# Decoder layer on one core: the relu of the index scores stays in its PSUM bank, and the weighted sum reads it from there

## The chip, the cores and the metric

One core of one Trainium2 chip runs the whole program. The metric is the device time of one launch in microseconds (us). The kernel before took 1060.78 us, the median of three runs (1059.88 to 1061.40). The profile comes from one further execution, of 1061.52 us.

## What is computed

One layer in float32: 512 tokens of width 1024 go through a SwiGLU feed-forward block, a token mixer of two head groups, and a second SwiGLU block. The change lies in the mixer's first group, where a small indexer scores every earlier key for every query and each query keeps its best 128 keys:

```python
idx_logits = jnp.einsum('bqhd,bsd->bqhs', qib, k_idx)       # 16 index heads of width 64
score = jnp.einsum('bqh,bqhs->bqs', wb, jax.nn.relu(idx_logits))
score = jnp.where(causal[None], score, -jnp.inf)
_, sel = lax.top_k(score, top_k)                            # top_k = 128
```

The first block of 128 queries sees no more than 128 keys, so it needs no scores. The blocks 1, 2 and 3 score 256, 384 and 512 keys.

## The kernel before

The program is written with pools of named tiles, and a scheduler puts the instructions of each engine into an order and adds the waits. Engines run their own queues in that order: TensorE (PE) the matmuls, ScalarE (ACT) activations, VectorE (DVE) elementwise work, GpSimd (POOL) part of the elementwise work, SyncE (SP) the issue of transfers. PSUM has eight banks of 128x512 float32, all handed out by one helper (`acc`, which is also `sc` and `tr`; line 77); a matmul group takes a free bank and must wait where none is free.

A float32 matrix product is made of three matmuls on operands split into a high and a low part (`mm3`, line 135). The weights are split by `split` (line 93): an ACT copy writes the high part (line 94), DVE or POOL subtracts it from the raw weights to get the low part (line 95). The set ON_VECTOR says which of these subtractions, and which additions of the rotary embedding, are DVE's; the others are POOL's.

The mixer's first part is written out by hand in the string ORDER: `q0` to `q7` project index queries for two heads each (`index_queries`), `s0` to `s7` rotate them and split them into stacked tiles (`rope`, lines 622 to 636, and `stack`, lines 644 to 654; four transfers on SP move quarters of the low part, line 639), `i0` to `i7` make the scores of two heads each (`index_heads`), `l0` to `l4` project the latents of the second head group (`latent`, lines 736 to 746), and `b` stands for rounds of the selection (`topk`).

For each of 16 heads and 3 blocks, so 48 times, `index_heads` does this:

- two matmuls put the scores of 128 queries against 256, 384 or 512 keys into a bank `p` (lines 707 and 708),
- ACT writes the relu of the bank into an SBUF tile `r`, one of four (line 710),
- DVE multiplies `r` by the head's weight per query and adds the sum so far, `score[i]`, which the trace calls idx (line 711). For the first head it adds the mask cmask instead.

The bank is free again when the relu is done. The tile `r` is free when the sum is done.

`topk` then takes the eight largest scores of each row (line 719) and replaces them (line 720), 16 rounds for the three blocks, all on DVE, and line 723 turns the result into a mask for the attention. `latent` reads its product three times: ACT writes the scaled high part (line 741), DVE the low part (line 742), ACT the squares for the norm (line 154). Line 872 is the first step of the attention's softmax.

Of the kernel before, what the change touches and what calls it, by code (L numbers as in the profile page):

```python
# [11 lines left out]
AF = mybir.ActivationFunctionType  # L12
# [561 lines left out]
def mixer(k, mp, mix, ids, xs, turn_rest, norm, tabs, g_q, g_kv, row_tile, out_done, on_token):  # L574
    nc = k.nc
# [3 lines left out]
    fr = lambda: pp.tile([P, T], F32, tag="r", name=k.name("r"), bufs=BUFS["pr"])  # L579
# [85 lines left out]
    wt = mp.tile([P, NT, 16], F32, tag="wt", name="wt", bufs=1)  # L665
    qst = lambda: mp.tile([P, T], F32R, tag="kf", name=k.name("qst"), bufs=8)
    score = {i: mp.tile([P, T], F32, tag="idx", name=f"idx_{i}", bufs=3)[:, :(i + 1) * P] for i in range(1, NT)}
# [32 lines left out]
    def index_heads(c, stacks):  # L700
        for j, s in enumerate(stacks):
            h = 2 * c + j
            for i in range(1, NT):
                n = (i + 1) * P
                p = k.sc()[:, :n]
                q = s[:, (i - 1) * P:i * P]
                nc.tensor.matmul(p, q, kih[:, :n], start=True, stop=False)
                nc.tensor.matmul(p, q, kil[:, :n], start=False, stop=True)
                r = fr()[:, :n]
                nc.scalar.activation(r, p, AF.Relu)  # L710
                nc.vector.scalar_tensor_tensor(out=score[i], in0=r, scalar=wt[:, i, h:h + 1],  # L711
                                               in1=cm(i) if h == 0 else score[i], op0=ALU.mult, op1=ALU.add)


# [124 lines left out]
    def values_b(j):  # L839
        wv = k.weights(ids["V"])  # L840
        for j in range(NT):
            p = k.acc()
            for a in range(2):
# [5 lines left out]

    do = dict(T=keys, c=norm_column, t=rest, r=norm_rows, k=index_keys, a=attention_keys, v=rest_out, w=lambda j: values(v.x2),  # L850
              e=lambda j: rotary_key(v.x2), q=index_queries, s=index_stack, i=lambda j: index_heads(j, stacks.pop(j)), l=latent,
              K=keys_b, R=keys_b_out, p=rotary_b, u=rotary_b_out, n=nope, A=queries_a, S=stack_a, V=values_b, b=background)
    for w in steps[:steps.index("|")]:
# [379 lines left out]
```

## Time and profile before

| | |
|---|---|
| median of three runs | 1060.78 us |
| profiled execution, whole | 1061.52 us |
| its span, first to last instruction | 1059.7 us |
| mean granted TensorE clock | 0.987 |
| PE busy, share of the span | 1016.4 us, 96% |
| DVE busy | 513.2 us, 48% |
| ACT busy | 384.3 us, 36% |
| POOL busy | 147.5 us, 14% |
| index scores, first matmul to last sum | 416.2 to 478.0 us |
| selection, line 719 to line 723 | 478.6 to 549.8 us |

The shares are means over stages that differ. Before 380 us and after 660 us the feed-forward blocks keep PE busy in nearly every slice; in between, the mixer loads DVE and POOL far more, and what bounds it has to be read from that stretch alone. A busy PE is no proof of a bound: an instruction's time there is modelled and overlaps the next one's. Rows in order of time merge neighbours of one group (a last field "x3" says three instructions) and give start, duration and, in brackets, the idle time just before and who ended it.

### The profile page before, as it was taken

The numbers are of one execution on the slowest core, as the hardware profiler recorded it, in microseconds if no ns is written. First come the engines' busy times: TensorE is split into PE (matmuls) and PEld (weight loads), VectorE is DVE, ScalarE is ACT, GpSimd is POOL, SyncE is SP. The second block draws the span as 40 slices with busy tenths as digits, with TensorE's granted clock in tenths as the row PEclk, the third lists the DMA queues.
The fourth block names the chain that finished last, engine by engine and source line by source line (L and its number), as shares of the span: only waits on it lengthen the run. The fifth ranks groups of instructions, "written<-read, shape, count | busy, mean of one in ns | idle before, by whom it ended". The sixth has DMA issues, their size and how long they took to land.

```text
span 1059.7 us, 12214 instructions
## 1 busy us (share of the span) xinstructions
PE 1016.4 (96%) x4726; PEld 829.8 (78%) x4726; DVE 513.2 (48%) x897; ACT 384.3 (36%) x689; POOL 147.5 (14%) x142
## 2 busy tenths in 40 slices
PE   6999999999999999889879999999999999999997
PEld 4888888888888888768755567888888888888886
DVE  6433333233332346989996767553333233333343
ACT  5422222122222335563466556442222211222232
POOL 1000000000000026625975122000000000000000
PEclk9999999999999999989988999999999999999999
DMA  8322332233313123333350001344323232222302
GB/s 278 120 80 81 118 119 80 80 99 109 111 60 97 40 80 109 114 92 98 98 174 15 2 19 43 102 138 124 113 80 119 80 113 86 80 83 98 119 0 80
DMA packets 83390, 98.84 MB, mean 93 GB/s; under 512 B 9026, under 2 KB 65474, under 8 KB 83332
## 3 DMA queue, kind: packets, MB, share of 16 engines
q1 hardware_dynamic: 83328, 98.06, 29.4%
q8 instruction: 37, 0.61, 0.2%
q14 instruction: 21, 0.17, 0.1%
q10 hardware_dynamic: 4, 0.00, 0.0%
HBM read 91.89 MB, written 2.10 MB: 89 GB/s over the span
## 4 chain that ended last, share of the span: by engine, by line
PE 80%; DVE 12%; issue 3%; ACT 3%; POOL 1%; DMA 1%; SPq 0%; POOLq 0%; ACTq 0%; DVEq 0%
PE ps L137 24%; PE ps L140 24%; PE ps L141 24%; DVE idx L720 2%; DVE s L719 2%; DVE idx L711 1%; PE ps L960 1%; DVE wl L95 1%; PE ps L998 1%; DVE p L892 1%; PE ps L993 1%; PE ps L957 1%; DVE p L872 1%; PE ps L982 1%; DVE f L626 0%
## 5 line engine op out<-in xcount | busy, mean ns | idle before, releaser
L94 ACT ACTIVATE wh<-raw 128x1024 fp32r<-128x1024 f32 (+4 forms) x154 | 140.1, 925 | 381.1 <-PE ps L140 298.9
L95 DVE TENSOR_TENSOR wl<-raw,wh 128x1024 fp32r<-128x1024 f32 (+1 forms) x122 | 145.5, 1196 | 266.2 <-ACT wh L94 265.9
L137 PE MATMUL ps<-xh,wh 128*128 128x512 f32 (+2 forms) x712 | 265.9, 378 | 5.1 <-DVE res L1137 1.7
L141 PE MATMUL ps<-xh,wl 128*128 128x512 f32 (+2 forms) x712 | 267.3, 377 | 1.2 <-POOL wl L95 0.9
L140 PE MATMUL ps<-xh,wh 128*128 128x512 f32 (+2 forms) x712 | 267.2, 377 | 0.5 <-DVE xh L95 0.5
L137 PEld LDWEIGHTS ps<-xh,wh 128*128 128x128 f32 x712 | 133.7, 189 | 29.6 <-DVE f L629 2.1
L141 PEld LDWEIGHTS ps<-xh,wl 128*128 128x128 f32 x712 | 134.6, 189 | 24.9 <-POOL wl L95 1.3
L140 PEld LDWEIGHTS ps<-xh,wh 128*128 128x128 f32 x712 | 134.5, 189 | 23.6 <-DVE xh L95 0.7
L137 PE MATMUL ps<-wh,h 128*128 128x512 f32 x272 | 105.9, 389 | 0.0
L140 PE MATMUL ps<-wl,h 128*128 128x512 f32 x272 | 105.8, 389 | 0.0
L141 PE MATMUL ps<-wh,h 128*128 128x512 f32 x272 | 105.8, 389 | 0.0
L95 POOL TENSOR_TENSOR wl<-raw,wh 128x512 fp32r<-128x512 f32 (+5 forms) x32 | 43.3, 1374 | 394.4 <-ACT wh L94 389.8
L334 DVE TENSOR_TENSOR t<-ps,t 128x512 f32<-128x512 f32 x44 | 30.4, 691 | 138.5 <-PE ps L141 138.5
L94 ACT ACTIVATE w<-raw 128x1024 fp32r<-128x1024 f32 x32 | 33.9, 1061 | 117.5 <-PE ps L140 117.5
L137 PE MATMUL ps<-xh,w 128*128 128x512 f32 x176 | 68.5, 389 | 0.0
L141 PE MATMUL ps<-xh,w 128*128 128x512 f32 x176 | 68.5, 389 | 0.0
L140 PE MATMUL ps<-xh,w 128*128 128x512 f32 x176 | 68.5, 389 | 0.0
L289 POOL TENSOR_TENSOR fr<-tot,mhalf 128x1 f32<-128x1 f32 x12 | 7.0, 582 | 417.9 <-DVE tot L1180 360.1
L140 PEld LDWEIGHTS ps<-wl,h 128*128 128x128 f32 x272 | 51.1, 188 | 10.6
L141 PEld LDWEIGHTS ps<-wh,h 128*128 128x128 f32 x272 | 51.1, 188 | 10.6
L137 PEld LDWEIGHTS ps<-wh,h 128*128 128x128 f32 x272 | 51.0, 188 | 10.6
L95 DVE TENSOR_TENSOR w<-raw,w 128x1024 fp32r<-128x1024 f32 x32 | 39.2, 1225 | 29.8 <-ACT w L94 29.8
(214 smaller groups left out, 1346.2 us busy)
## 6 DMA issues: line engine op xcount, KB each, us to landing
raw<-in_w_up_dram SPq DMA_DIRECT2D x22, 1024.0 KB, 5.3
raw<-in_w_gate_dram SPq DMA_DIRECT2D x21, 1024.0 KB, 5.3
raw<-in_w_down_dram SPq DMA_DIRECT2D x20, 1024.0 KB, 5.0
raw<-in_w_in_dram SPq DMA_DIRECT2D x8, 1024.0 KB, 5.2
raw<-in_w_out_dram SPq DMA_DIRECT2D x4, 1024.0 KB, 5.8
res<-in_x_dram SPq DMA_DIRECT2D x4, 512.0 KB, 6.0
raw<-in_w_down_dram SPq DMA_DIRECT2D x4, 512.0 KB, 3.8
raw<-in_w_ukv_dram SPq DMA_DIRECT2D x2, 1024.0 KB, 4.9
```

Source lines behind the costliest of these rows:

```text
L94: i = self.nc.scalar.activation(hi, src, AF.Copy)
L95: (lo_engine or self.nc.vector).tensor_tensor(out=lo, in0=src, in1=hi.bitcast(F32), op=ALU.subtract)
L137: i = mm(out, wh, xh, start=first, stop=False)
L140: mm(out, wh, xl, start=False, stop=False)
L141: return i, mm(out, wl, xh, start=False, stop=last)
L334: nc.vector.tensor_tensor(out=u, in0=pu, in1=g, op=ALU.mult)
L711: nc.vector.scalar_tensor_tensor(out=score[i], in0=r, scalar=wt[:, i, h:h + 1], in1=cm(i) if h == 0 else score[i], op0=ALU.mult, op1=ALU.add)
L719: nc.vector.max(out=m8, in_=score[i])
L720: nc.vector.match_replace(out=score[i], in_to_replace=m8, in_values=score[i], imm_value=TAKEN)
L872: nc.vector.tensor_tensor_reduce(out=e, in0=p[:, :n], in1=bias, scale=1.0, scalar=-3.0e38, op0=ALU.add, op1=ALU.max, accum_out=mx[:, c:c + 1])
L892: nc.vector.tensor_scalar(out=e, in0=e, scalar1=rc[:, c:c + 1], scalar2=None, op0=ALU.mult)
L957: nc.tensor.transpose(p[:, i * P:(i + 1) * P], probs[i][:, j * P:(j + 1) * P], k.ident)
```

## The change

The tile `r` is gone. The relu writes back into the bank that it reads, and the weighted sum takes its first operand from that bank. The bank is therefore free only when the sum is done. The same 48 relus and 48 sums run. The pool's four `r` buffers remain allocated (one call, line 657, stays).

```diff
--- before.py
+++ after.py
@@ -706,9 +706,8 @@
                 q = s[:, (i - 1) * P:i * P]
                 nc.tensor.matmul(p, q, kih[:, :n], start=True, stop=False)
                 nc.tensor.matmul(p, q, kil[:, :n], start=False, stop=True)
-                r = fr()[:, :n]
-                nc.scalar.activation(r, p, AF.Relu)
-                nc.vector.scalar_tensor_tensor(out=score[i], in0=r, scalar=wt[:, i, h:h + 1],
+                nc.scalar.activation(p, p, AF.Relu)
+                nc.vector.scalar_tensor_tensor(out=score[i], in0=p, scalar=wt[:, i, h:h + 1],
                                                in1=cm(i) if h == 0 else score[i], op0=ALU.mult, op1=ALU.add)
```

Line numbers behind line 709 are smaller by one after the change. The scheduler orders the queues anew. On TensorE the order of the index part is the same, but the matmuls that open a bank wait for another engine. Below are the widest score of one index head and all three of the next, at the end of a run of 12 scores that closes with a latent projection; ps is a bank, kih and kil the split index keys, qst a stacked query tile, and the brackets name the queues whose semaphore is waited for (Activation is ACT). Before:

```order
L707 MATMUL ps_3361<-kih,qst_3198 128x512 [waits Activation_49]
L708 MATMUL ps_3361<-kil,qst_3198 128x512
L707 MATMUL ps_3367<-kih,qst_3199 128x256 [waits DMAHW1_49,DMAHW0_49,Activation_49]
L708 MATMUL ps_3367<-kil,qst_3199 128x256
L707 MATMUL ps_3373<-kih,qst_3199 128x384 [waits Activation_49]
L708 MATMUL ps_3373<-kil,qst_3199 128x384
L707 MATMUL ps_3379<-kih,qst_3199 128x512 [waits Activation_49]
L708 MATMUL ps_3379<-kil,qst_3199 128x512
L137 MATMUL ps_3389<-xh_2392,wh_3145 128x512 [waits Activation_49]
```

After:

```order
L707 MATMUL ps_3329<-kih,qst_3180 128x512 [waits DVE_49]
L708 MATMUL ps_3329<-kil,qst_3180 128x512
L707 MATMUL ps_3334<-kih,qst_3181 128x256 [waits DMAHW7_49,DMAHW0_49,DVE_49]
L708 MATMUL ps_3334<-kil,qst_3181 128x256
L707 MATMUL ps_3339<-kih,qst_3181 128x384 [waits Activation_49]
L708 MATMUL ps_3339<-kil,qst_3181 128x384
L707 MATMUL ps_3344<-kih,qst_3181 128x512 [waits DVE_49]
L708 MATMUL ps_3344<-kil,qst_3181 128x512
L137 MATMUL ps_3353<-xh_2392,wh_3127 128x512 [waits DVE_49]
```

The rows are the same matmuls in the same places. Before, a bank is handed on when ACT is done with it, after the change in most places when DVE is.

On ScalarE, from the last scores of the third pair of heads to the first of the fourth (f and qst are the rotated queries and their stack, wh the high part of weights). Before:

```order
L94 ACTIVATE wh_3100<-raw_3098 128x1024
L710 ACTIVATE r_3089<-ps_3086 128x384
L648 ACTIVATE qst_3135<-f_3129 128x384
L650 ACTIVATE qst_3136<-f_3129 128x384
L710 ACTIVATE r_3095<-ps_3092 128x512
L94 ACTIVATE wh_3145<-raw_3098 128x1024
L648 ACTIVATE qst_3182<-f_3174 128x384
L650 ACTIVATE qst_3183<-f_3174 128x384
L94 ACTIVATE wh_3278<-raw_3276 128x1024
L710 ACTIVATE r_3243<-ps_3240 128x256
```

After:

```order
L709 ACTIVATE ps_3075<-ps_3075 128x512
L648 ACTIVATE qst_3117<-f_3111 128x384
L650 ACTIVATE qst_3118<-f_3111 128x384
L94 ACTIVATE wh_3082<-raw_3080 128x1024
L94 ACTIVATE wh_3127<-raw_3080 128x1024
L648 ACTIVATE qst_3164<-f_3156 128x384
L650 ACTIVATE qst_3165<-f_3156 128x384
L94 ACTIVATE wh_3254<-raw_3252 128x1024
L709 ACTIVATE ps_3222<-ps_3222 128x256
```

Before, the last relu of the third pair stands behind a weight split and behind the copies of queries; after, it stands ahead of both, as no buffer `r` has to come free.

On VectorE at the same place (idx_2657 to idx_2659 are the three blocks' sums, wl the low part of weights, h the low part of queries). Before:

```order
L711 SCALAR_TENSOR_TENSOR idx_2657<-r_3083,wt,idx_2657 128x256
L95 TENSOR_TENSOR wl_3101<-raw_3098,wh_3100 128x1024
L711 SCALAR_TENSOR_TENSOR idx_2658<-r_3089,wt,idx_2658 128x384
L711 SCALAR_TENSOR_TENSOR idx_2659<-r_3095,wt,idx_2659 128x512
L626 TENSOR_TENSOR f_3192<-ps_3104,tab_2644 128x384
L628 TENSOR_TENSOR f_3193<-ps_3104,tab_2645 64x384
L629 TENSOR_TENSOR f_3193<-ps_3104,tab_2645 64x384
L626 TENSOR_TENSOR f_3210<-f_2842,tab_2648 128x512
L649 TENSOR_TENSOR h_3184<-f_3174,qst_3182 128x384
```

After:

```order
L710 SCALAR_TENSOR_TENSOR idx_2659<-ps_3060,wt,idx_2659 128x512
L710 SCALAR_TENSOR_TENSOR idx_2657<-ps_3065,wt,idx_2657 128x256
L710 SCALAR_TENSOR_TENSOR idx_2658<-ps_3070,wt,idx_2658 128x384
L710 SCALAR_TENSOR_TENSOR idx_2659<-ps_3075,wt,idx_2659 128x512
L95 TENSOR_TENSOR wl_3083<-raw_3080,wh_3082 128x1024
L626 TENSOR_TENSOR f_3174<-ps_3086,tab_2644 128x384
L628 TENSOR_TENSOR f_3175<-ps_3086,tab_2645 64x384
L629 TENSOR_TENSOR f_3175<-ps_3086,tab_2645 64x384
L626 TENSOR_TENSOR f_3192<-f_2842,tab_2648 128x512
L649 TENSOR_TENSOR h_3166<-f_3156,qst_3164 128x384
```

The weight split (line 95) stood ahead of the last two sums of that pair and now stands behind them; the rotary steps (lines 626 to 629) follow in the same order. On SyncE, two loads of weights (the last latent's, and the query weights of the second group) now stand behind two and four more of the copies of line 639. All other queues keep their order but for swaps of neighbours.

## Rows read from the trace of the kernel before

**Rows 1.** chain of work that ended last, whole span, shares by engine.

```profile
PE 80%; DVE 12%; issue 3%; ACT 3%; POOL 1%; DMA 1%; SPq 0%; POOLq 0%; ACTq 0%; DVEq 0%
```

**Rows 2.** busy us per engine in stretches; PEclk, DMA share, GB/s close each row.

```profile
472.00:500.00 28.00, 27.95 (x136) 23.29 (x134) 28.00 (x72) 12.97 (x26) 11.01 (x11) 1.00 0.30 97
...
500.00:520.00 20.00, 17.58 (x85) 14.24 (x86) 20.00 (x55) 7.23 (x13) 19.36 (x15) 1.00 0.37 113
...
520.00:550.00 30.00, 24.85 (x110) 18.88 (x108) 29.94 (x63) 17.34 (x26) 27.17 (x23) 0.96 0.48 140
```

**Rows 3.** VectorE groups by form, 420 to 480 us: busy us, mean ns of one, idle.

```profile
L711 DVE SCALAR_TENSOR_TENSOR idx<-r,wt,idx 128x512 f32<-128x512 f32 x15 | 14.8, 985 | 0.0
...
L711 DVE SCALAR_TENSOR_TENSOR idx<-r,wt,idx 128x384 f32<-128x384 f32 x15 | 11.9, 796 | 0.1
...
L711 DVE SCALAR_TENSOR_TENSOR idx<-r,wt,idx 128x256 f32<-128x256 f32 x15 | 10.0, 667 | 0.0
...
L742 DVE SCALAR_TENSOR_TENSOR lat<-ps,g_q_lat,lat 128x512 fp32r<-128x512 f32 x2 | 1.5, 747 | 2.0 <-ACT lat L741 2.0
...
L711 DVE SCALAR_TENSOR_TENSOR idx<-r,wt,cmask 128x512 f32<-128x512 f32 x1 | 0.7, 744 | 0.0
...
L711 DVE SCALAR_TENSOR_TENSOR idx<-r,wt,cmask 128x384 f32<-128x384 f32 x1 | 0.6, 611 | 0.0
...
L711 DVE SCALAR_TENSOR_TENSOR idx<-r,wt,cmask 128x256 f32<-128x256 f32 x1 | 0.5, 485 | 1.4 <-ACT r L710 1.4
```

**Rows 4.** VectorE in order of time, 425 to 444 us: start, duration, what.

```profile
425.79 2.65 DVE L711 SCALAR_TENSOR_TENSOR idx<-r,wt,idx 128x512 f32<-128x512 f32 x2
...
428.83 1.96 DVE L711 SCALAR_TENSOR_TENSOR idx<-r,wt,idx 128x384 f32<-128x384 f32 x3
...
434.50 3.20 DVE L711 SCALAR_TENSOR_TENSOR idx<-r,wt,idx 128x384 f32<-128x384 f32 x3
...
439.58 4.16 DVE L711 SCALAR_TENSOR_TENSOR idx<-r,wt,idx 128x384 f32<-128x384 f32 x2
```

**Rows 5.** GpSimd in order of time, two weight splits.

```profile
440.48 2.71 POOL L95 TENSOR_TENSOR wl<-raw,wh 128x1024 fp32r<-128x1024 f32 x1
...
469.04 2.40 POOL L95 TENSOR_TENSOR wl<-raw,wh 128x1024 fp32r<-128x1024 f32 x1 [7.34 <-ACT wh L94]
```

**Rows 6.** VectorE in order of time, 459 to 473 us.

```profile
459.99 7.55 DVE L711 SCALAR_TENSOR_TENSOR idx<-r,wt,idx 128x256 f32<-128x256 f32 x12
...
469.57 0.75 DVE L742 SCALAR_TENSOR_TENSOR lat<-ps,g_q_lat,lat 128x512 fp32r<-128x512 f32 x1 [2.03 <-ACT lat L741]
...
470.24 3.05 DVE L711 SCALAR_TENSOR_TENSOR idx<-r,wt,idx 128x256 f32<-128x256 f32 x2
```

**Rows 7.** who waited for whom, 415 to 480 us: total us, times, longest.

```profile
ACT r L710 <- DVE idx L711: 9.5, 8, 3.3
...
PE ps L707 <- DMA qst<-h: 4.0, 2, 3.0
...
PEld ps L707 <- ACT r L710: 2.2, 3, 1.2
```

**Rows 8.** TensorE matmuls in order of time, four rows of 457 to 513 us.

```profile
457.38 0.55 PE L707 MATMUL ps<-kih,qst 128*128 128x256 f32 x1 [2.99 <-DMA qst<-h]
...
459.05 0.69 PE L707 MATMUL ps<-kih,qst 128*128 128x384 f32 x1 [0.90 <-ACT r L710]
...
472.37 0.50 PE L137 MATMUL ps<-xh,wh 128*128 128x512 f32 x1
...
512.97 0.50 PE L137 MATMUL ps<-xh,wh 128*128 128x512 f32 x1 [1.54 <-ACT wh L94]
```

**Rows 9.** who waited for whom, 480 to 500 us.

```profile
ACT f L154 <- DVE lat L742: 9.6, 3, 3.4
```

**Rows 10.** ScalarE group by form, 420 to 480 us, the widest relu.

```profile
L710 ACT ACTIVATE r<-ps 128x512 f32<-128x512 f32 x16 | 9.7, 605 | 4.8 <-DVE idx L711 3.9 <-PE ps L708 0.8
```

**Rows 11.** SyncE queue in order of time, one row.

```profile
447.41 2.41 SPq L639 DMA_DIRECT2D qst<-h  x4
```

## The prediction

> **What bounds the kernel now.** I started from the chain of waits that ended last: PE carries 80% of it and DVE 12% [rows 1]. The reader is to see that a DVE change can only pay where DVE stands in that chain, so next I looked at busy time by stretch [rows 2]. From 472 to 500 us DVE is busy 28.00 of 28.00 us, to 520 us 20.00 of 20.00, to 550 us 29.94 of 30.00. PE is just as full until 500 us (27.95), then has gaps; POOL is nearly full from 500 us on (19.36 of 20, 27.17 of 30). So DVE bounds the selection, with PE and POOL close behind, and time saved on DVE ahead of 478 us can move the whole rest of the program, as far as those two follow.
>
> Then I asked what DVE's weighted sums cost, by form [rows 3]. The sums of the first head take 744, 611 and 485 ns for 512, 384 and 256 columns. The other 45, with the same work, average 985, 796 and 667 ns. In order of time the long ones stand together [rows 4]: two sums from 439.58 us take 4.16 us, and the POOL split that runs from 440.48 us takes 2.71 us of it [rows 5]. DVE and POOL evidently hold each other up when both read two operands from SBUF. The low part of a latent is the same DVE operation, with its first operand in PSUM: its row at 469.57 us takes 0.75 us although a POOL split runs from 469.04 us for 2.40 us; the two sums right behind it, with both operands in SBUF, take 3.05 us [rows 5, 6].
>
> **The change, part by part.** *The sums.* With `p` in place of `r` a sum has one operand in SBUF and one in PSUM, like that latent row, and I take it that POOL no longer holds it up. Saved on DVE: 15 x (985 - 744) + 15 x (796 - 611) + 15 x (667 - 485) ns = 3.6 + 2.8 + 2.7 = 9.1 us [rows 3]. Reading PSUM costs little by itself: 747 ns for the latent rows against 744 for the sum of that width [rows 3], 3 ns, 0.1 us in 48 sums.
>
> The Trainium skill speaks against this (Perfetto Trace Analysis, Optimizing Scalar/DVE Operations): it gives a DVE instruction about 60 ns of access overhead on SBUF and 125 on PSUM. By that page the 48 sums would cost 3.1 us more, and the saving would be an estimated 6.0 us instead of 9.1. The two rows show no such difference.
>
> *Where the saving falls.* Neighbours start about 0.08 us before the previous one ends (469.57 + 0.75 against 470.24 [rows 6]), so I count that off. Ahead of 457 us the four groups [rows 4] are too long by 2.65 - (744 + 485 - 80 ns) = 1.50, 1.96 - 1.68 = 0.28, 3.20 - 1.68 = 1.52 and 4.16 - 1.28 = 2.88: together 6.2 us. The remaining 2.9 us lie behind, of which 3.05 - (485 + 611 - 80 ns) = 2.0 us are the pair at 470.24 [rows 6].
>
> *What PE does with it.* At 457.38 us PE has waited 2.99 us for copied queries [rows 7, 8], whose rotation is queued on DVE behind those sums. So PE starts 6.2 us earlier. From there it is nearly gapless, so what it loses, it keeps.
>
> *The banks.* A bank now stays taken until DVE's sum. In the first run of 12 scores a latent product holds one bank, so seven are open and the eighth score takes the bank of the first. PE got it at 459.05, after 0.90 us of waiting for a relu [rows 8]; now it waits for the first of the 12 sums, 459.99 + 0.49 = 460.48 us [rows 3, 6]: 1.4 us lost. In the second run the sums start at 470.24; three take 485 + 611 + 744 - 240 ns = 1.60 us. The projection that follows the 12 scores is the thirteenth taker of eight banks and waits for the fifth sum: 470.24 + 1.60 + 0.40 + 0.61 = 472.85, against 472.37 now [rows 8]: 0.5 us. ACT's wait for `r` (9.5 us in 8 waits [rows 7]) goes. What it held up were relus, and DVE was busy with the sums ahead of them, so I cost it at nothing beyond DVE's own gain.
>
> *The relu into PSUM.* No row shows ACT writing PSUM. The widest relu takes 605 ns into SBUF, 9.7 us for all 16 of them [rows 10]; that row is the nearest there is. Half and double of it are my ends, -0.3 and +0.6 us a relu. DVE works off earlier sums meanwhile, so either reaches the path as one relu's latency where a run of scores begins, not 48 times. I take 0 and keep -0.3 and +0.6 us.
>
> *Moved steps.* Two weight loads go behind two and four more copies on SP, 0.6 us each (2.41 us for four [rows 11]): 1.2 and 2.4 us later. In the list of waits of that stretch, of which [rows 7] shows three, no weight split waits for a transfer, so I take 0 and keep 2.4 us as the upper end. The moved weight split and relus trade places with neighbours on engines that do the same work in sum: 0.
>
> *The sum.* At 469.57 us DVE waits for PE's projection, so its gain is PE's: 6.2 - 1.4 = 4.8 us. With the pair's 2.0 it is 6.8 at the end of the sums. PE is ahead by 6.2 - 1.4 - 0.5 = 4.3. In the selection ACT's squares wait 9.6 us in three times for DVE to read the same latents [rows 9], so DVE comes 3.2 us late to each and can move up 6.8 - 4.3 = 2.5 us against PE without waiting. At 512.97 PE waits 1.54 us for a weight split [rows 8], which comes earlier with DVE, so PE gains up to 4.3 + 1.5 = 5.8 there. The stage ends 5.8 to 6.8 us earlier; I take 6.3. What follows is taken as unchanged. The profiled execution gives 1061.52 - 6.3 = 1055.2; it lies 0.74 us above the median, so the forecast for the median is **1054.5 us**.
>
> **The rivals.** *The banks bite in every run.* A rule of the Trainium skill points here (PSUM — Partial Sum Buffer, Summary: rules for kernel authors): evacuate promptly, as the space is tight. The rows show relus holding PE up already, 2.2 us in three waits [rows 7]. If the three runs of six scores ahead of 457 us also lose 1.4 us each, 6.2 shrinks to 2.0; DVE ends at 2.0 - 1.4 + 2.0 = 2.6, PE at 2.0 - 1.9 + 1.5 = 1.6. Time: 1060.78 - 1.6 = 1059.2. Against it: a run of six and a projection fit into eight banks.
>
> *Slower: POOL still holds the sums, and only the banks are felt.* If the sum so far (in SBUF, read and written) is enough to be held, nothing is saved. PE loses 1.4 us, and in the second run the fifth sum ends at 470.24 + 3.05 + (744 + 485 + 611 - 240 ns) = 474.9, 2.5 us late: 3.9 in all. Less the 1.54 us that PE waits anyway at 512.97, 2.4 us remain: 1063.2. It decides as soon as DVE saves less than PE loses. Against it stands the latent row at 469.57 [rows 6], held not at all.
>
> *The sum is dearer from PSUM.* The forecast falls below 0.2%, 2.1 us, if each sum costs (6.3 - 2.1) / 48 = 88 ns more. Two rows of 747 against 744 ns speak against it, though only at one width. With half of that, 44 ns, 2.1 us of the gain go: 1056.6. By the page's 65 ns, an estimate, it would be 3.1 us less gain, 1057.6.
>
> **How the numbers follow.** A change below 0.2%, about 2.1 us, is what a measurement of this kernel can hardly tell from none. The forecast gets 0.69, the banks 0.15, the slower rival 0.10, the dearer sum 0.06. Below 1060.78 - 2.1 = 1058.7 I count 0.66 of the forecast, 0.04 of the dearer sum and 0.03 of the banks: faster 0.73. The slower rival has 0.10, and 0.17 stays for no difference. The range reaches down to the full 9.1 us (1051.7) and the 0.7 us by which a quicker relu and a run without bank waits could go on, to 1051.0; up it takes in the banks' rival at 1059.2 and half of the late loads' 2.4 us, to 1060.5. The slower rival is left out.
>
> **What would show it.** Right: the 48 sums average near 744, 611 and 485 ns whatever POOL does, DVE busy on them falls from 37 to 29 us or so; ACT's waits for the sums are gone; PE waits for DVE's sums where it takes banks, about 2 us in all; the last sum ends 6 to 7 us earlier, and so does the selection. Wrong: sums still beyond 1 us beside a POOL split, PE waits for sums of more than 4 us, or a selection that ends early while the attention starts no earlier, held by POOL's steps for it.

## The result, and the profile after

After the change the kernel took **1053.93 us** (median of six runs, 1052.90 to 1054.78) beside 1060.67 us for the kernel before on the same chip: a ratio of 0.9936, 95% interval 0.9923 to 0.9949, so 6.7 us less. The forecast was 1054.5 us and faster. The profiled execution took 1054.78 us with a span of 1053.0 us; 6.7 us against 6.3 in the sum.

The weighted sums by form, on VectorE, 415 to 475 us (busy us, mean ns of one, idle before):

```profile
L710 DVE SCALAR_TENSOR_TENSOR idx<-ps,wt,idx 128x512 f32<-128x512 f32 x15 | 11.2, 746 | 0.0
L710 DVE SCALAR_TENSOR_TENSOR idx<-ps,wt,idx 128x384 f32<-128x384 f32 x15 | 9.2, 612 | 0.0
L710 DVE SCALAR_TENSOR_TENSOR idx<-ps,wt,idx 128x256 f32<-128x256 f32 x15 | 7.2, 479 | 0.0
```

They answer to [rows 3]: 985, 796 and 667 ns have become 746, 612 and 479, what the first head's sums took all along. The three groups fall from 36.7 to 27.6 us.

VectorE in order of time, from a rotary step at 442 us to the first step of the selection:

```profile
442.51 2.70 DVE L628 TENSOR_TENSOR f<-f,tab 64x512 f32<-64x512 f32 x1
...
454.17 6.39 DVE L710 SCALAR_TENSOR_TENSOR idx<-ps,wt,idx 128x256 f32<-128x256 f32 x12
465.32 0.75 DVE L741 SCALAR_TENSOR_TENSOR lat<-ps,g_q_lat,lat 128x512 fp32r<-128x512 f32 x1 [4.76 <-ACT lat L740]
465.99 6.39 DVE L710 SCALAR_TENSOR_TENSOR idx<-ps,wt,idx 128x256 f32<-128x256 f32 x12
472.29 1.47 DVE L718 MAX8 s<-idx 128x8 f32<-128x256 f32 x3
```

And GpSimd in the same stretch:

```profile
441.95 2.72 POOL L95 TENSOR_TENSOR wl<-raw,wh 128x1024 fp32r<-128x1024 f32 x1
...
454.80 1.01 POOL L649 TENSOR_TENSOR h<-f,qst 128x384 fp32r<-128x384 f32 x1
464.79 2.38 POOL L95 TENSOR_TENSOR wl<-raw,wh 128x1024 fp32r<-128x1024 f32 x1 [8.98 <-ACT wh L94]
```

Before, the two runs of twelve sums took 7.55 us [rows 6] and, from 470.24 us, 8.48. Both now take 6.39 us. A POOL split ran into the start of the second as it did before, and it no longer shows. The step at 442.51, with both operands in SBUF, is still held beside a split: 2.70 us, the same as before. The first MAX8 starts at 472.29 us, 6.35 earlier than before (478.64).

Where PE takes a bank, it now waits for sums. TensorE matmuls in order of time, rows of 442 to 470 us:

```profile
442.62 0.39 PE L137 MATMUL ps<-xh,wh 128*128 128x512 f32 x1
...
449.82 0.50 PE L707 MATMUL ps<-kih,qst 128*128 128x512 f32 x1 [0.38 <-DVE idx L710]
...
450.95 0.39 PE L707 MATMUL ps<-kih,qst 128*128 128x256 f32 x1 [0.39 <-DVE idx L710]
...
452.52 0.38 PE L707 MATMUL ps<-kih,qst 128*128 128x256 f32 x1
454.71 0.60 PE L707 MATMUL ps<-kih,qst 128*128 128x384 f32 x1 [1.69 <-DVE idx L710]
...
463.68 0.28 PE L707 MATMUL ps<-kih,qst 128*128 128x256 f32 x1
...
466.52 0.44 PE L707 MATMUL ps<-kih,qst 128*128 128x384 f32 x1 [0.32 <-DVE idx L710]
...
469.01 0.39 PE L137 MATMUL ps<-xh,wh 128*128 128x512 f32 x1
```

The row at 452.52 is the one that stood at 457.38 before, behind 2.99 us of waiting for copied queries [rows 8]; that wait is gone. The next score, at 454.71, starts as the first of the twelve sums ends (454.17 + 0.49). All such waits, 415 to 475 us (total us, times, longest), with those of PE's weight loads (PEld) and the one that DVE now has itself:

```profile
PEld ps L707 <- DVE idx L710: 7.0, 14, 1.9
DVE lat L741 <- ACT lat L740: 4.8, 1, 4.8
...
PE ps L707 <- DVE idx L710: 2.8, 4, 1.7
```

A weight load can wait while an earlier matmul still runs, so its 7.0 us are not all lost time.

No row is left for ACT waiting on sums, where 9.5 us stood [rows 7]. The widest relu into PSUM takes what it took into SBUF [rows 10], 603 against 605 ns (ScalarE by form, 415 to 475 us):

```profile
L709 ACT ACTIVATE ps<-ps 128x512 f32<-128x512 f32 x16 | 9.7, 603 | 0.6 <-PE ps L708 0.6
```

In the selection ACT's squares wait 2.7 us for the latents where they waited 9.6 [rows 9] (waits, 480 to 500 us):

```profile
ACT f L154 <- DVE lat L741: 2.7, 2, 1.9
```

PE and DVE are both full there, as before [rows 2] (busy us by stretch: PE, PEld, DVE, ACT, POOL):

```profile
472.00:500.00 28.00, 28.00 (x141) 23.77 (x140) 28.00 (x84) 10.23 (x19) 15.24 (x14) 1.00 0.36 113
```

The first softmax step of the attention starts at 542.9 us (549.7 before), and from there the rest takes 510.1 us (510.0 before). So the gain is made by 472 us and handed on whole.

### The profile page after: what moved, and what is told of

Its sections match the earlier page's. It is cut to its first block, busy times and chain, and to the rows that moved or that the text cites. A ratio compares the mean times of both kernels' runs of the same rounds, so it can differ in the third digit from the quotient of the medians.

```text
span 1053.0 us, 12210 instructions
## 1 busy us (share of the span) xinstructions
PE 1015.4 (96%) x4726; PEld 829.6 (79%) x4726; DVE 505.0 (48%) x897; ACT 383.0 (36%) x689; POOL 147.2 (14%) x142
## 4 chain that ended last, share of the span: by engine, by line
PE 80%; DVE 11%; issue 3%; POOL 2%; ACT 2%; DMA 0%; SPq 0%; POOLq 0%; DVEq 0%; ACTq 0%
PE ps L137 24%; PE ps L140 24%; PE ps L141 24%; DVE idx L719 2%; DVE s L718 1%; PE ps L959 1%; DVE wl L95 1%; DVE idx L710 1%; POOL wl L95 1%; PE ps L997 1%; DVE p L891 1%; PE ps L992 1%; PE ps L956 1%; PE ps L981 1%; POOL f L634 0%
```

## The experiments

A table of all of them first, each kernel's time against the kernel before on the same chip. The last three columns come from each kernel's own trace: "stage" runs from the start of the first weighted sum to the end of the last, "sums" is DVE's busy time on the 48 of them, "rest" is the stage without them, that is what DVE spends on other work and on waiting. (A sum's row overlaps its neighbours by some 0.07 us, which "sums" counts twice, 2.6 to 3.2 us in a kernel.) In e9 alone the scheduler put four instructions of the selection, 1.5 us by their rows, ahead of the last sums, so its stage and its rest are that much too long beside the others.

| kernel | median us | ratio to before, 95% interval | stage | sums | rest |
|---|---|---|---|---|---|
| before | 1060.7 to 1061.2 | 1 | 57.1 | 38.6 | 18.6 |
| the change | 1053.93 | 0.9936 (0.9923 to 0.9949) | 50.8 | 29.4 | 21.4 |
| the change again | 1054.28 | 0.9934 (0.9921 to 0.9948) | 50.8 | 29.1 | 21.7 |
| e1, six tiles r | 1062.90 | 1.0024 (1.0014 to 1.0033) | 59.0 | 39.9 | 19.1 |
| e2, bank for pairs 0 to 3 | 1052.34 | 0.9926 (0.9913 to 0.9940) | 50.4 | 32.5 | 18.0 |
| e3, bank for pairs 4 to 7 | 1062.88 | 1.0019 (1.0010 to 1.0027) | 57.3 | 35.4 | 21.8 |
| e4, bank but for pairs 4 and 7 | 1050.38 | 0.9901 (0.9888 to 0.9915) | 48.4 | 30.5 | 17.9 |
| e5, no relu | 1053.72 | 0.9921 (0.9905 to 0.9938) | 51.6 | 29.2 | 22.4 |
| e6, before with load on POOL | 1062.31 | 1.0012 (1.0003 to 1.0021) | 60.0 | 42.2 | 17.9 |
| e7, change with load on POOL | 1057.19 | 0.9963 (0.9950 to 0.9976) | 53.9 | 29.2 | 24.6 |
| e8, bank but for pair 4 | 1052.97 | 0.9923 (0.9911 to 0.9936) | 49.2 | 30.3 | 18.9 |
| e9, bank but for pairs 4 and 5 | 1054.89 | 0.9936 (0.9924 to 0.9949) | 52.7 | 32.4 | 20.3 |

A pair of heads makes six scores (two heads, three blocks). Pairs 4 and 7 are the first run of twelve, pairs 5 and 6 the second. Three of the expectations below (e4, e8, e9) count three scores to a pair; it is six, and in e4 the whole first run goes through `r`.

**Was it the wait for a tile `r`?** (e1)

```diff
-    fr = lambda: pp.tile([P, T], F32, tag="r", name=k.name("r"), bufs=BUFS["pr"])
+    fr = lambda n: pp.tile([P, n], F32, tag=f"r{n}", name=k.name("r"), bufs=2)
...
-                r = fr()[:, :n]
+                r = fr(n)
```

> The relu still goes to SBUF, into two tiles r for each of the three widths, six in all where there were four. My theory (sums with both operands in SBUF are held up by POOL's splits): the sums stay near 985, 796 and 667 ns and the time stays within 1.5 us of before. Rival (the gain came from ACT no longer waiting for an r, 9.5 us in eight waits): those waits shrink and the kernel is 4 to 7 us faster than before.

ACT's wait for an `r` did shrink, from 9.5 to 3.8 us, and nothing was gained: the time rose by 2 us, a little more than the 1.5 us that the theory allowed, and the sums stayed long (39.9 us). PE's waits for the stacked queries grew to 6.8 us for ACT's copies and 6.2 for transfers (waits, 415 to 485 us), where the kernel before has 3.4 in the same list and 4.0 [rows 7]; why the queries come later there was not followed:

```profile
PEld ps L706 <- ACT qst L650: 6.8, 2, 4.1
PE ps L706 <- DMA qst<-h: 6.2, 2, 3.7
```

So the rival falls: the waits went down by 5.7 us and bought nothing.

**Where the gain and the price lie.** (e2, e3) The relu stays in the bank for one half of the pairs only, `c` being the pair; the first added line is e2's, the second e3's:

```diff
-                r = fr()[:, :n]
+                r = p if c < 4 else fr()[:, :n]
+                r = p if c > 3 else fr()[:, :n]
```

> The relu stays in the bank for the first four pairs of heads only (the runs of six scores, ahead of the two runs of twelve); the last four pairs go through r as before. Theory: about 6.2 of the 9.1 us of shorter sums lie here and no bank is waited for, so 5 to 7 us faster than before, near the whole change. Rival (banks bite in runs of six too, or the gain comes from the late pairs): 0 to 3 us faster.

> The counterpart: the relu stays in the bank for the last four pairs only (two runs of twelve scores each). Theory: 2.9 us of shorter sums, of which the waits for banks take about 2 back: 0 to 2 us faster than before. Rival (the late pairs carry the gain, since DVE bounds the stage that follows at once): 3 to 6 us faster.

e2 alone is as quick as the whole change (8.5 us less than before; the intervals overlap). That is more than the 5 to 7 us expected. It saves 6.1 us of sums, and its stage is 6.7 us shorter, as expected; in its trace the part from the first softmax on, where nothing was edited, is 2.8 us shorter too (507.2 us instead of 510.0), and why is not shown. e3 saves 3.2 us of sums and its stage is no shorter, since "rest" grows by 3.2. Its PE row in order of time shows the price:

```profile
459.91 0.69 PE L707 MATMUL ps<-kih,qst 128*128 128x384 f32 x1 [2.67 <-DVE idx L711]
```

The eighth score of the first long run waits 2.67 us for the first sum of that run. In time e3 came out 2.0 us slower than before, outside what either theory expected: in its trace the part from the first softmax on takes 512.4 us instead of 510.0, at a lower granted clock (0.96 from 20 to 60 us after that softmax, 1.00 before the change). What lowers it there was not followed.

**Give back only the banks that PE waits for.** (e4)

```diff
-                r = fr()[:, :n]
+                r = fr()[:, :n] if c in (4, 7) else p
```

> As the change, but the two pairs of heads that open the first run of twelve (six scores) go through r, so that their banks are free after the relu. Theory: PE's waits for DVE's sums there (1.7 and 0.4 us) go, their sums are held by POOL at most a little, and the kernel is 0.5 to 2 us faster than the change. Rival (DVE alone sets the end and PE's waits for banks are slack): the same as the change or up to 1.5 us slower, by the longer sums.

1050.38 us: **this version beats both kernels**, its interval (0.9888 to 0.9915) lying below that of the change. It gained more than the 0.5 to 2 us over the change that were expected: 3.5 us by the medians, of which 2.4 lie in the stage. PE's matmuls at the same scores, in order of time:

```profile
449.37 0.39 PE L707 MATMUL ps<-kih,qst 128*128 128x256 f32 x1 [0.40 <-DVE idx L711]
...
451.52 0.44 PE L707 MATMUL ps<-kih,qst 128*128 128x384 f32 x1
...
459.70 0.28 PE L707 MATMUL ps<-kih,qst 128*128 128x256 f32 x1
```

The row at 451.52 is the eighth score; it waits for nothing, where the change waited 1.69 us. From the fourth score of this run to the first of the next PE takes 459.70 - 449.37 = 10.33 us; with the change 463.68 - 450.95 = 12.73. VectorE in order of time:

```profile
452.60 7.57 DVE L711 SCALAR_TENSOR_TENSOR idx<-r,wt,idx 128x256 f32<-128x256 f32 x12
461.34 0.75 DVE L742 SCALAR_TENSOR_TENSOR lat<-ps,g_q_lat,lat 128x512 fp32r<-128x512 f32 x1 [1.17 <-ACT lat L741]
462.00 6.39 DVE L711 SCALAR_TENSOR_TENSOR idx<-ps,wt,idx 128x256 f32<-128x256 f32 x12
468.30 1.47 DVE L719 MAX8 s<-idx 128x8 f32<-128x256 f32 x3
```

The first run's sums are held again (7.57 us instead of 6.39), and that costs nothing, since DVE waits for the next latent behind them anyway: 4.76 us with the change, 1.17 here. The second run, behind which nothing waits, keeps its 6.39.

Of the 2.40 us that PE gains, 1.69 are the wait. Most of the rest must lie with the granted clock. Before, in stretches of 2 us (the third number from the end is the granted clock):

```profile
454.00:456.00 2.00, 0.39 (x2) 0.00 (x0) 2.00 (x5) 0.60 (x1) 0.00 (x0) 0.87 0.09 22
456.00:458.00 2.00, 0.62 (x2) 0.50 (x2) 1.43 (x3) 1.73 (x3) 0.00 (x0) 0.50 0.33 86
...
460.00:462.00 2.00, 2.00 (x8) 1.81 (x7) 2.00 (x3) 1.19 (x3) 1.62 (x2) 0.50 0.50 68
462.00:464.00 2.00, 2.00 (x9) 1.62 (x9) 2.00 (x5) 1.68 (x4) 0.00 (x0) 0.92 0.95 340
```

With the change:

```profile
454.00:456.00 2.00, 1.29 (x4) 1.07 (x5) 2.00 (x5) 2.00 (x6) 1.73 (x2) 0.71 0.14 33
456.00:458.00 2.00, 2.00 (x8) 1.80 (x7) 2.00 (x5) 1.42 (x4) 0.00 (x0) 0.50 0.24 57
458.00:460.00 2.00, 2.00 (x9) 1.62 (x9) 2.00 (x5) 0.71 (x2) 0.00 (x0) 0.94 0.29 75
```

In e4:

```profile
454.00:456.00 2.00, 2.00 (x9) 1.59 (x9) 2.00 (x4) 1.14 (x4) 0.33 (x1) 1.00 0.30 72
456.00:458.00 2.00, 2.00 (x10) 1.64 (x10) 2.00 (x5) 1.87 (x4) 0.00 (x0) 1.00 0.34 86
```

Before the change the clock stood at 0.50, the lower level of 1.2 GHz, from within 454 to 456 us until past 462, while PE waited and after it had waited 2.99 and 0.90 us [rows 8]. With the change it fell again, behind the wait of 1.69 us, and was back after 458 us. In e4 PE does not wait there, and the clock stays at its full 2.4 GHz.

**Is the relu on the path?** (e5)

```diff
-                r = fr()[:, :n]
-                nc.scalar.activation(r, p, AF.Relu)
-                nc.vector.scalar_tensor_tensor(out=score[i], in0=r, scalar=wt[:, i, h:h + 1],
+                nc.vector.scalar_tensor_tensor(out=score[i], in0=p, scalar=wt[:, i, h:h + 1],
```

> The relu is left out: the sum reads the raw scores in the bank (this part of the computation is left out). Theory: the relus, some 23 us of ACT, are hidden behind DVE's earlier sums, and a bank is still held to the sum; within 1.5 us of the change. Rival (the relu's write into PSUM or its place ahead of the sum is on the path): 2 us or more faster than the change.

1053.72 us, 0.2 us from the change by the medians. The four runs spread from 1050.85 to 1055.08 us and the intervals overlap, so the time alone could hide a gain of an us or two; but the stage is no shorter in the trace (51.6 against 50.8 us). So 23.7 us of ACT work (9.7 + 7.9 + 6.1 us in the three forms of the change's relus) can go without a gain that these runs show: the relus are hidden, wherever they are written.

**Is it POOL that holds the sums?** (e6, e7) Two additions for each stacked tile of the last four pairs, to `dum`, an SBUF tile that nothing reads; e6 on the kernel before, e7 on the change:

```diff
+        if c > 3:
+            for s in stacks:
+                f = s.bitcast(F32)
+                for _ in range(2):
+                    nc.gpsimd.tensor_tensor(out=dum, in0=f[:, :256], in1=f[:, :256], op=ALU.add)
```

> Before, with 16 additions of 128x256 in SBUF put on POOL during the last four pairs of heads (their result is not used), about 0.65 us each by the nearest rows, 10 us in all. Theory: DVE's sums with both operands in SBUF are held up by them; the sums of the late pairs grow beyond 985, 796 and 667 ns in the mean and the time grows by 3 to 8 us. Rival (the sums were long for another reason than POOL): unchanged sums, and the time within 1.5 us of before.

> The change with the same 16 additions on POOL. Theory: the sums stay at 746, 612 and 479 ns; what grows is only DVE's work with two operands in SBUF (rotary steps, splits), so 0 to 3 us slower than the change and clearly less than the same load costs before. Rival (POOL holds an operand in PSUM as well): sums grow, and the load costs the same 3 to 8 us.

The sums answer plainly. e6, VectorE in order of time, the two runs of twelve:

```profile
457.89 10.37 DVE L717 SCALAR_TENSOR_TENSOR idx<-r,wt,idx 128x256 f32<-128x256 f32 x12
...
468.84 11.42 DVE L717 SCALAR_TENSOR_TENSOR idx<-r,wt,idx 128x256 f32<-128x256 f32 x12
```

Its POOL, one row of that time:

```profile
465.23 4.19 POOL L706 TENSOR_TENSOR dum<-qst 128x256 f32<-128x256 f32 x5 [1.78 <-DMA qst<-h]
```

e7, the same two runs on VectorE:

```profile
456.23 6.39 DVE L716 SCALAR_TENSOR_TENSOR idx<-ps,wt,idx 128x256 f32<-128x256 f32 x12
...
469.07 6.38 DVE L716 SCALAR_TENSOR_TENSOR idx<-ps,wt,idx 128x256 f32<-128x256 f32 x12
```

With both operands in SBUF the load stretches the runs from 7.55 and 8.48 us to 10.37 and 11.42; with one in PSUM they stay at 6.39 and 6.38. The times do not answer so plainly, and here the expectations failed: the load cost the kernel before only 1.1 us (3 to 8 expected). It cost the change 3.3 us by the medians, or 2.8 if each is first set against the kernel before that ran beside it: the upper end of the 0 to 3 expected, and more than the same load cost before, where less was expected. In e7 none of it is in the sums; "rest" grew by 3.2 us. Some 2.1 us of it are there before the first run of twelve starts (456.23 against 454.17 us). Part of that are DVE's steps with both operands in SBUF, as the theory had it; the addition of line 635, with the change and in e7, on VectorE in order of time:

```profile
446.42 0.68 DVE L635 TENSOR_TENSOR f<-f,f 128x512 f32<-128x512 f32 x1
```

```profile
445.00 2.77 DVE L635 TENSOR_TENSOR f<-f,f 128x512 f32<-128x512 f32 x1
```

The other 1.0 us is lost between the two runs, which start 469.07 - 456.23 = 12.84 us apart instead of 465.99 - 454.17 = 11.82. PE waits 1.66 us for the first sum, as with the change (1.69), and from there to the next run it waits for nothing. But the granted clock stays low for longer; in e7, one stretch of 2 us (with the change it was back after 458 us):

```profile
460.00:462.00 2.00, 2.00 (x6) 1.57 (x5) 2.00 (x5) 0.84 (x2) 0.16 (x1) 0.50 0.53 173
```

Why e6, whose stage is 2.9 us longer, ends only 1.1 us later was not settled; in its trace, of 1061.30 us, the stage starts 1.4 us earlier than before, and the part from the first softmax on is 1.4 us shorter (508.6 against 510.0).

**How few banks must be given back early?** (e8, e9, and the change once more) The first added line is e8's, the second e9's:

```diff
-                r = fr()[:, :n]
+                r = fr()[:, :n] if c == 4 else p
+                r = fr()[:, :n] if c in (4, 5) else p
```

> As the change, but only the pair of heads that opens the first run of twelve (three scores) goes through r. Theory: the three banks that TensorE needs first come free with the relu, so its wait of 1.7 us for the first sum of that run goes, and with it the 3 us of halved granted clock behind it; about 3 us faster than the change, like the version with two pairs in r (1050 to 1051 us). Rival (what that version won came from the second pair too): between the two, 1052 to 1053 us, with a wait of about 1 us for a later sum.

> As the change, but the opening pair of each of the two runs of twelve (three scores each) goes through r. Theory: TensorE's wait of 0.32 us in the second run goes too, but its three sums are held a little; within 1 us of the version with only the first of these pairs in r. Rival (the banks of the second run cost more than their wait shows): 1 to 2 us faster than that version.

> The change itself once more, beside the two versions: 1053 to 1055 us, with a wait of 1.7 us for a sum near 454 us and a granted clock of half right behind it. Rival (the lower clock there was chance, and the faster versions only met a better execution): no lower clock near 455 us, and a time within 1 us of theirs.

The change again took 1054.28 us and showed the same wait of 1.69 us, with a granted clock of 0.50 behind it, so this is no chance of one execution. e8 took 1052.97 us, as its rival had it, though by other waits. Its interval overlaps those of the change and of e4; its stage (49.2 us) lies between theirs (50.8 and 48.4). Its PE in order of time, the twelfth score and the projection behind the run:

```profile
454.59 0.50 PE L707 MATMUL ps<-kih,qst 128*128 128x512 f32 x1 [0.54 <-ACT f L154]
...
455.76 0.50 PE L137 MATMUL ps<-xh,wh 128*128 128x512 f32 x1 [0.44 <-ACT r L710]
```

Both wait for ACT, which holds a bank until it has squared a latent or done a late relu: 1 us of the 1.69 comes back in another place. e9 took 1054.89, 1.9 us more than e8, which neither its theory nor its rival had; the two intervals overlap, so the times alone do not settle it. Its second run on VectorE, first four sums and last one:

```profile
463.05 4.11 DVE L711 SCALAR_TENSOR_TENSOR idx<-r,wt,idx 128x256 f32<-128x256 f32 x4
...
472.14 0.73 DVE L711 SCALAR_TENSOR_TENSOR idx<-ps,wt,idx 128x512 f32<-128x512 f32 x1
```

A POOL split holds sums there again, and DVE has no slack behind this run: sums of 32.4 us instead of 30.3, to save PE a wait of 0.32 us.

## Why the prediction was right

**The sums (9.1 us).** Right, 36.7 - 27.6 = 9.1, and for its reason: e6 and e7 show that POOL's work lengthens a sum with both operands in SBUF and not one with an operand in PSUM. The slower rival assumed the opposite and falls with them. The dearer sum falls too: 746, 612 and 479 ns against the 744, 611 and 485 of unheld sums from SBUF [rows 3]. The rule of the Trainium skill (Perfetto Trace Analysis, Optimizing Scalar/DVE Operations), by which PSUM would have added an estimated 65 ns to each, is not borne out: these rows differ by 6 ns at most, at three widths.

**Where the saving falls.** The prediction lets PE start the seventh score of the first long run 6.2 us earlier. It started 457.38 - 452.52 = 4.86 us earlier, so this step was 1.3 us too high: PE no longer waits for the queries at all. But for two waits of 0.4 us for banks it comes there straight from its own matmuls, and the projection ahead of that run began only 445.39 - 442.62 = 2.77 us earlier. TensorE before, two rows in order of time:

```profile
445.39 0.50 PE L137 MATMUL ps<-xh,wh 128*128 128x512 f32 x1 [1.63 <-DVE f L629]
...
467.93 0.28 PE L707 MATMUL ps<-kih,qst 128*128 128x256 f32 x1
```

It hardly shows behind that, because the eighth score waits for DVE's first sum, and that came 459.99 - 454.17 = 5.8 us earlier. The eighth score starts 459.05 - 454.71 = 4.3 us earlier; 6.2 - 1.4 = 4.8 was the forecast. The latent behind it comes 469.57 - 465.32 = 4.25 us earlier (4.8), the second run adds 8.48 - 6.39 = 2.1 (2.0), and the last sum ends 478.72 - 472.38 = 6.3 us earlier (6.8). (The 478.0 us in the table of the profile before are the start of that sum.)

**The banks (1.4 + 0.5 us).** The mechanism was right, and so was the first place: the eighth score waits 1.69 us. In the second run it was not the projection that waited for the fifth sum but again the eighth score that waited for the first (465.99 + 0.48 = 466.47 us), for 0.32 us. In all that run loses 0.9 us instead of 0.5: from its first score to the projection PE takes 469.01 - 463.68 = 5.33 us, before 472.37 - 467.93 = 4.44. What is not in the 0.32 probably lies in the waits of the weight loads. The step that a run of six and a projection fit into eight banks, by which the rival of banks that bite in every run was turned down, was wrong by 0.38 + 0.39 us: the sums of that run stand in DVE's queue behind rotary steps, and the next run's third and fourth score wait for them. These two waits lie ahead of the 1.69. Without them PE would have come to the eighth score sooner and waited longer there, as that sum starts when DVE comes to it; so the waits do not simply add up. What PE kept is seen at the projection behind the second run: it starts 472.37 - 469.01 = 3.4 us earlier, where the forecast had 4.3. With the first run's banks freed by the relu (e4) the stage is 2.4 us shorter than the change's and the kernel 3.5 us quicker (1053.93 - 1050.38); that the other 1.1 us come from the banks too is not shown. So the rule of the Trainium skill to evacuate promptly (PSUM — Partial Sum Buffer, Summary: rules for kernel authors) does bear on this kernel, in the first run of twelve above all; elsewhere little: the second run loses 0.9 us, and e2, which holds banks in the runs of six alone, paid 0.4 us twice.

**The relu (0).** Right: 603 against 605 ns, and the stage of e5, without it, is no shorter. **ACT's wait for `r` (0).** Right, by e1. **Moved steps (0).** In the selection one weight split on ACT waits 4.2 us for its transfer where it waited 2.7, but starts 3.4 us earlier all the same (488.24 against 491.60 us), and the selection was none the later.

**The end (6.3 us).** The stage ended 6.8 us earlier, the upper end of the 5.8 to 6.8 given, and the 510 us behind it stayed, as assumed. The forecast came out 0.6 us too high. Two small errors cancel: PE kept 0.9 us less than forecast, and it did not hold the selection back, so that DVE carried its 6.3 us through it, and 0.5 us more that the selection itself saved (70.6 us from its first step to the first softmax, 71.1 before). So the time came out closer than its steps, and that is in part luck. (The upper end of the range, 1059.2 and half of 2.4 us, adds up to 1060.4 and not 1060.5.)

**What the sum left out** is the granted clock. It was low before the change, in and behind the waits of 2.99 and 0.90 us, and was low again after it, behind the 1.69 us. From the eighth score to the latent the two kernels take the same (469.57 - 459.05 = 10.52, 465.32 - 454.71 = 10.61 us), so the omission cancelled. In e4 it does not, and such a sum would have missed part of its gain.

## What to carry to other kernels

Where VectorE and GpSimd work at the same time, look for VectorE operations whose mean lies well above that of the same form when GpSimd is idle; leaving one of two SBUF operands in PSUM made them independent of it here, for no extra time per instruction. The price is a bank held until VectorE gets to it, and it falls above all where a run of bank takers is longer than the number of banks and VectorE is behind. So do it by place and not throughout: keep the early release where TensorE waits for a bank and VectorE has slack behind the run (e4), and hold the bank where VectorE bounds what follows.

## What was not expected of the hardware

- A wait of TensorE can cost more than its length: behind 1.69 us of waiting the granted clock was 0.50 for some 3 us, and it stayed at 1.00 in the version without that wait (e4). Behind the shorter waits of e8, 0.54 and 0.44 us, it stayed at 1.00 as well.
- The rotary step at 442.51 us, 64x512 with both operands in SBUF, takes 2.70 us beside a GpSimd split; the same form behind it (line 629) takes 0.68. One held operation costs as much as several sums.
- Profiled executions differ by up to 1.6 us already before the first weighted sum (it starts between 420.02 and 421.60 us), without an edit there. In the kernel before the granted clock was 0.66 from 410 to 415 us, in e2 it was 1.00, with PE equally full. That is why the stage is measured here from its own start.
